# First entry with tokens on partitions, outputs finished at set steps, and squares and scale rows later at three entries

## The chip, the cores and the metric

The kernel runs on one core of one Trainium2 chip. The metric is the device time of one execution in microseconds. TensorE multiplies matrices (PE in the profile, PEld for its weight loads), VectorE (DVE) and GpSimd (POOL) do elementwise work, ScalarE (ACT) activations and copies, and SyncE (SP) issues nearly all transfers.

## The reference

A hybrid decoder layer on x of 1024 tokens by 1024 features, all float32, cut to its lines:

```python
x = x + 0.5 * swiglu(rms_norm(x, ffn1_norm), ffn1_w_gate, ffn1_w_up, ffn1_w_down)   # D_FF = 2816
h = rms_norm(x, mix_norm)
fq, fk, fv, f_logit, sq, sk, sv, g_fox, g_sb = split_columns(h @ w_in)
...                      # two causal token mixers, 8 heads of 64 each
merged = sigmoid(g_fox) * (y_fox @ w_branch_fox) + sigmoid(g_sb) * (y_sb @ w_branch_sb)
x = x + merged @ w_out
x = x + 0.5 * swiglu(rms_norm(x, ffn2_norm), ffn2_w_gate, ffn2_w_up, ffn2_w_down)
x = x + sigmoid(rms_norm(x, ple_norm) @ w_ple_gate) * (p @ w_ple_proj)
```

where `rms_norm(x, g) = x * rsqrt(mean(x*x, axis=-1) + 1e-6) * g`, and `swiglu` is `(silu(h @ w_gate) * (h @ w_up)) @ w_down`.

## The kernel before

**Layout.** x is handed over transposed, so that features lie on the 128 partitions (8 blocks k) and tokens along the free axis, in two halves of 512. Every operand of a product is split into a rounded high part (a ScalarE copy into fp32r) and a low part (a VectorE subtraction), and a product is three passes high-high, high-low, low-high: 12 matmuls of 128x512 for four blocks. The split of weights is `prep(n, m)`; its ScalarE and VectorE steps are in `split`.

**Products with combinations.** A stage with 2x2 blocks (feature halves by token halves) is done with seven products in place of eight. `make_up` does this for the two feed-forwards, the gates of the mixer and the last stage (the gated layer embedding, called PLE here). For weight block n there are products (n, 1) to (n, 7); B[1] and B[2] are the normalised operand of token half 0, `"12"` and 3 that of half 1, and 5, 6, 7, 4 are sums and differences, built by `combo_a` and `combo_b` (scale half 1 and split it), `combo_t`/`combo_l` (5), `combo_u`/`combo_s` (6, and 7), `combo_d`/`combo_e` (4). Block 0 is done without combinations (`plain(f, half, parts)`), while these are built. `up_order` is the fixed list of products; `products(F)` does what stands before it: (1,1), (1,2), plain for half 1. Then steps s = 0, 1, 2, ... follow the list, which begins (2,1), (1,5), (2,2), (1,6), (1,7), (2,6), (2,5), (1,3), (2,7), (1,4), (3,1), (2,4), (3,2). For the last stage it goes on with (3,6), (3,5), (3,7), (2,3), (3,3), (3,4), s = 13 to 18. At each step come the product, `evict` (bank copied or added into a result tile `E[n]`, activation), `begin(s)` and `prep` of the product four steps ahead.

**Order.** These stages stand in a manual schedule: each engine carries out its instructions in the order of the program text, and an instruction that waits holds up all behind it on its engine. Buffers come from named pools (`BUFS`: GF, RN, Q, KH, KL, Y, X 2 each, T 6, H and PT 4, WL and WH 3); a new tile waits until the last use of the one whose buffer it takes, also where that use stands later in the text of another engine.

**Norms.** `norm_sq` squares a feature block on ScalarE and adds it to an accumulator, on GpSimd mostly (line 187); `norm_sum` sums over partitions by matmuls with a column of ones (line 196) and takes the power -0.5 on GpSimd; `norm_row` (line 208) turns the result into a row over all partitions by transposes; `norm_mul` scales. At the first entry (`first_entry`) half 0's squares are summed by matmuls directly (line 190). At the other three entries (mixer, second feed-forward, last stage) squares and scaling are woven into the last down products by `up_step`, and `up_first` runs the first plain products.

**Last stage.** `ple_start` (lines 1539 to 1636): `fetch` loads p's projection and x for a 128-row tile into two buffers, `finish(n, i, ...)` multiplies, adds and sends out (lines 1559 to 1561). Finishes are put in a list `lag` and done at the next `evict`, after its own steps; each finish then fetches the next tile. `E[n]` takes buffers GF and RN for every n, two of each; line 1583 is the copy of (n,1) into GF, line 1585 that of (n,6), 1588 the add of (n,7).

Of the kernel before, what the change touches and what calls it, by code (L numbers as in the profile page):

```python
# [36 lines left out]
def tile_hybrid_decoder_layer(  # L37
    ctx: ExitStack,
    tc: tile.TileContext,
    x, p, ffn1_norm, ffn1_w_gate, ffn1_w_up, ffn1_w_down, mix_norm, w_in, forget_bias,  # L40
# [118 lines left out]
    gains = cp.tile([P, 4, KD], F32, name="gains")  # L159
    for i, gain in enumerate((ffn1_norm, mix_norm, ffn2_norm, ple_norm)):  # L160
        nc.scalar.dma_start(gains[:, i, :], gain[0])
# [14 lines left out]
    def norm_sq(N, k, eng=nc.gpsimd, ps=None):  # L176

        q = N["q"]
        if ps is None and "acc" not in N:
            d = N["acc"] = q["t"][0][:, N["half"], :]  # L180
            nc.scalar.activation(d, N["x"][:, k, :], AF.Square, scale=D ** -0.5)
            return
        q["n"] += 1
        d = q["t"][1][:, q["n"] % 2, :]
        nc.scalar.activation(d, N["x"][:, k, :], AF.Square, scale=D ** -0.5)  # L185
        if ps is None:
            eng.tensor_add(N["acc"], N["acc"], d)  # L187
            return
        for t in range(4):
            pe(nc.tensor.matmul(ps[:, t:t + 1], d[:, t * P:(t + 1) * P], ones1[:], start=(k == 0 and t == 0), stop=(k == KD - 1), skip_group_check=True))  # L190
# [37 lines left out]
    def norm_low(N, k, eng=nc.vector):  # L228
        B = N["B"][k // 4]
        eng.tensor_sub(B[:, 1, k % 4, :], N["x"][:, k, :], f(B[:, 0, k % 4, :]))  # L230

# [47 lines left out]
    def up_step(N, X, dst, F, i, t):  # L279
# [19 lines left out]
        elif i == 6:  # L299
            finished(X, dst, 1, t)  # L300
            if t == 0:
                norm_mul(N[0], 7)
            for k in ((0, 1, 2), (3, 4), (5, 6), (7,))[t]:
                norm_high(N[0], k)
            norm_sq(N[1], t, nc.vector if t == 3 else nc.gpsimd)
            for k in ((0, 1, 2), (3, 4), (5, 6), (7,))[t]:
                norm_low(N[0], k)

    def up_first(N, F):
# [12 lines left out]
        F.plain(1, 0)  # L322
        combos(F)
        products(F)
# [142 lines left out]
    def make_up(N, src, nm_, tags, first_fn, first_done=None, over=None):  # L467
# [17 lines left out]
        def plain(f_, half, parts=(0, 1), out=True):  # L485
# [5 lines left out]
            for kh in parts:  # L491
                hl, rb = hls[0, ((1, 2), (5, 4))[f_][kh]], B[("12", 3)[kh]] if half else whole(N[0]["B"][kh])
                for a, b in ((0, 0), (1, 0), (0, 1)):
                    for k in range(4):
                        pe(nc.tensor.matmul(ps[:], hl[:, a, k, :], rb[b](k), start=(i == 0), stop=(i == 23)))  # L495
                        i += 1
# [38 lines left out]
        def product(n, m, cols=slice(0, 512)):  # L535
# [9 lines left out]
            for a, b in ((0, 0), (0, 1), (1, 0)):  # L545
                for k in range(4):
                    pe(nc.tensor.matmul(ps[:, cols], hl[:, a, k, :], B[m][b](k)[:, cols], start=(first and i == 0), stop=(final and i == 11), skip_group_check=True))  # L547
                    i += 1
            return ps

        def whole(t):
            return lambda k: t[:, 0, k, :], lambda k: t[:, 1, k, :]

        def home(m):
            tag = tags["B"][m]
            if isinstance(tag, str):
                return whole(slot(tag, [P, 2, 4, 512], F32R))
            t = [slot(x_, [P, 2, 512], F32R) for x_ in tag]
            return lambda k: t[k // 2][:, k % 2, :], lambda k: t[2 + k // 2][:, k % 2, :]

        def xk(half, k):
            return norm_at(N[half], k)

        def high(m, k, src):
            nc.scalar.copy(B[m][0](k), src)

        def low(m, k, src, eng=nc.vector):
            eng.tensor_sub(B[m][1](k), src, f(B[m][0](k)))

        def combo_a(k):  # L570

            if k == 0:
                B[1], B[2] = (whole(t) for t in N[0]["B"])
                B[3] = home(3)
                B["12"] = home("12")
            norm_mul(N[1], k)
            norm_mul(N[1], k + 4)
            high("12", k, xk(1, k))
            high(3, k, xk(1, k + 4))

        def combo_b(k, eng=None):
            if eng is not None:
                low("12", k, xk(1, k), eng)
            else:
                low(3, k, xk(1, k + 4))

        def combo_t(k):

            if k == 0:
                B[5] = home(5)  # L590
            nc.vector.tensor_sub(xk(0, k), xk(1, k), xk(0, k))
            high(5, k, xk(0, k))

        def combo_l(k):
            low(5, k, xk(0, k))

        def combo_u(k):
            nc.vector.tensor_sub(xk(1, k), xk(1, k + 4), xk(1, k))
            nc.vector.tensor_sub(xk(1, k + 4), xk(1, k + 4), xk(0, k))
            if k == 0:  # L600
                B[6] = home(6)
            high(6, k, xk(1, k + 4))

        def combo_s(k, m):

            if m == 6:
                low(6, k, xk(1, k + 4))
                return
            if k == 0:
                B[7] = home(7)  # L610
            high(7, k, xk(1, k))
            low(7, k, xk(1, k))

        def combo_d(k):
            nc.vector.tensor_sub(xk(1, k), xk(0, k + 4), xk(1, k + 4))

        def combo_e(k):
            if k == 0:
                B[4] = home(4)
            high(4, k, xk(1, k))  # L620
            low(4, k, xk(1, k))
# [538 lines left out]
    def mix_start():  # L1160
# [47 lines left out]
        def begin(i, X):  # L1208
            if not Xs:
                Xs.extend(X)  # L1210
            up_begin(N, X, 1, F, i)

        def end():
# [17 lines left out]
            hT.extend([lambda a, k: B0[k // 4][:, a, k % 4, :], lambda a, k: B1[k // 4][a](k % 4)])  # L1231
# [163 lines left out]
    X = [slot("X", [P, KD, 512]) for _ in range(2)][::-1]  # L1395
# [3 lines left out]
    def first_entry(F):  # L1399

        def load_x(half):
            for k in range(KD):
                nc.sync.dma_start(X[half][:, k, :], xs[k, :, half * 512:half * 512 + 512])

        claim(X[1])
        load_x(0)
        nc.scalar.activation(stat([P, 1], "ss")[:], mhalf[:, 0:1], AF.Silu)
        F.load(0)
        load_x(1)
        F.load(1)  # L1410
        q = scratch()
        N.append(norm_begin(X[0], 0, 0, scratch()))
        N.append(norm_begin(X[1], 0, 1, q, ("Q", "Q", "KH", "KL")))
        ps = bank("sc")
        for k in range(KD):
            norm_sq(N[0], k, ps=ps)
        norm_pow(N[0], ps)
        norm_row(N[0], bank("av"))
        F.prep(0, 1)
        F.prep(0, 5)  # L1420
        for k in range(4):
            norm_mul(N[0], k)
            norm_high(N[0], k)
        for k in range(4):
            norm_low(N[0], k)
            norm_sq(N[1], k)
        for k in range(4, 8):
            norm_mul(N[0], k)
            norm_high(N[0], k)
        F.prep(0, 2)  # L1430
        F.prep(0, 4)
        for k in range(4, 8):
            norm_low(N[0], k)
        for k in range(4, 8):
            norm_sq(N[1], k, nc.gpsimd if k < 6 else nc.vector)
        F.plain(0, 0, (0,), False)
        F.plain(1, 0, (0,), False)
        F.plain(0, 0, (1,))
        norm_sum(N[1], bank("sc"))
        F.prep(1, 1)  # L1440
        F.prep(1, 2)
        F.sums(1, nc.vector)
        F.plain(1, 0, (1,))
        norm_row(N[1], bank("av"))
        F.prep(1, 5)
        F.load(2)
        combos(F)
        products(F)
# [222 lines left out]
```

## Time and profile before

| what | us |
|---|---|
| median of 3 runs (2272.24 to 2272.86) | 2272.28 |
| the profiled execution | 2271.59 |
| its span in the trace | 2269.9 |
| TensorE busy in the span | 2224.8 |
| first plain product starts | 23.11 |
| last TensorE product starts | 2262.34 |

Rows of the order of time read: start, length, engine, line, operation, output <- inputs, shape, how many were merged into the row, and in brackets the idle time before it and who ended it. SPq and ACTq are transfers being issued.

### The profile page before, as it was taken

How to read it: one execution, taken by the hardware profiler on the slowest of the kernel's cores; microseconds unless marked ns; L12 is line 12 of the kernel's file. 1: busy time of each engine (PE TensorE's matmuls, PEld its weight loads, DVE VectorE, ACT ScalarE, POOL GpSimd, SP SyncE). 2: the span in 40 equal slices, each digit the busy share in tenths (PEclk: the TensorE clock that was granted, in tenths of full speed). 3: DMA queues.
4: the chain of work that ended last, by engine and by line, in shares of the span. 5: the costliest groups of instructions: out<-in, count | busy, mean ns of one | idle time of the engine just before them, and what ended most of it. 6: DMA issues, size and time to landing. Idle time of an engine off the chain costs nothing.

```text
span 2269.9 us, 30559 instructions
## 1 busy us (share of the span) xinstructions
PE 2224.8 (98%) x11218; PEld 1888.9 (83%) x11218; DVE 1525.1 (67%) x2354; ACT 1000.0 (44%) x1791; POOL 832.1 (37%) x789
## 2 busy tenths in 40 slices
PE   7999999999999999999999999999999999999997
PEld 6888888888888898999898888887888888888886
DVE  5854545497888334666678885889655555778797
ACT  4433333343455435555566663245333333434444
POOL 2244444310021335566556664521544353200120
PEclk9999999999999999999999999999999999999999
DMA  4223232484332425333324466741423232655325
GB/s 139 79 96 113 93 116 93 153 314 150 127 133 79 136 87 148 93 94 84 88 54 97 117 200 204 259 149 56 139 79 130 79 131 79 249 198 189 130 96 201
DMA packets 197477, 298.04 MB, mean 131 GB/s; under 512 B 29000, under 2 KB 109128, under 8 KB 197328
## 3 DMA queue, kind: packets, MB, share of 16 engines
q1 hardware_dynamic: 196752, 296.08, 39.6%
q8 instruction: 88, 1.44, 0.3%
q14 instruction: 61, 0.50, 0.1%
q10 hardware_dynamic: 576, 0.02, 0.0%
HBM read 196.14 MB, written 83.13 MB: 123 GB/s over the span
## 4 chain that ended last, share of the span: by engine, by line
PE 84%; DVE 9%; ACT 2%; issue 2%; DMA 1%; POOL 0%; SPq 0%; DVEq 0%; ACTq 0%; POOLq 0%
PE ps L547 39%; PE ps L447 18%; PE ps L770 7%; PE ps L778 5%; PE ps L1373 4%; PE ps L1111 3%; PE ps L495 2%; PE ps L1085 2%; PE ps L1027 1%; PE ps L1026 1%; DVE H L106 1%; PE ps L932 1%; DVE H L230 1%; DVE PT L1093 1%; DVE X L221 1%
## 5 line engine op out<-in xcount | busy, mean ns | idle before, releaser
L447 PE MATMUL ps<-H,H 128*128 128x512 f32 x2184 | 498.1, 389 | 1.9 <-DVE X L455 1.2
L447 PEld LDWEIGHTS ps<-H,H 128*128 128x128 f32 x2184 | 409.3, 188 | 87.7 <-issue 3.0
L547 PE MATMUL ps<-H,WL 128*128 128x512 f32 x1152 | 273.5, 391 | 6.9 <-ACT GF L1585 6.8
L547 PEld LDWEIGHTS ps<-H,WL 128*128 128x128 f32 x1152 | 217.0, 189 | 53.2 <-ACT GF L1585 7.2
L187 POOL TENSOR_TENSOR PT<-PT,PT 128x512 f32<-128x512 f32 x41 | 55.3, 1348 | 425.2 <-ACT PT L185 424.1
L547 PE MATMUL ps<-H,Q 128*128 128x512 f32 x636 | 150.8, 389 | 0.0
L547 PEld LDWEIGHTS ps<-H,Q 128*128 128x128 f32 x636 | 119.4, 188 | 24.8
L455 DVE SCALAR_TENSOR_TENSOR X<-ps,X 128x512 f32<-128x512 f32 x168 | 108.5, 685 | 46.8 <-PE ps L447 46.7
L547 PE MATMUL ps<-X,WL 128*128 128x512 f32 (+1 forms) x588 | 138.7, 385 | 0.6 <-ACT RN L1611 0.6
L547 PE MATMUL ps<-H,PT 128*128 128x512 f32 x540 | 129.1, 389 | 0.6 <-DVE RN L1588 0.6
L547 PEld LDWEIGHTS ps<-X,WL 128*128 128x128 f32 x588 | 108.9, 188 | 22.8 <-ACT RN L1611 0.8
L139 POOL TENSOR_TENSOR WL<-RAW,WH 128x512 fp32r<-128x512 f32 (+1 forms) x84 | 98.3, 1192 | 68.3 <-ACT WH L129 43.6
L1093 DVE TENSOR_TENSOR PT<-ps,PT 128x512 fp32r<-128x512 f32 (+1 forms) x160 | 100.0, 627 | 31.0 <-ACT PT L1087 30.3
L547 PEld LDWEIGHTS ps<-H,PT 128*128 128x128 f32 x540 | 101.2, 188 | 21.9 <-DVE RN L1588 1.0
L770 PE MATMUL ps<-WH,H 128*128 128x256 f32 x768 | 116.1, 288 | 0.8 <-ACT RN L835 0.8
L778 PE MATMUL ps<-H,WH 128*128 128x512 f32 x384 | 114.9, 406 | 0.0
L1111 PE MATMUL ps<-PT,X 128*128 128x256 f32 (+1 forms) x640 | 102.4, 286 | 6.4 <-DVE PT L1093 5.5
L1087 ACT CAST PT<-ps 128x512 fp32r<-128x512 f32 (+1 forms) x160 | 87.1, 548 | 43.3 <-PE ps L1085 42.1
L1111 PEld LDWEIGHTS ps<-PT,X 128*128 128x128 f32 x640 | 90.3, 190 | 16.7 <-DVE PT L1093 10.3
L770 PEld LDWEIGHTS ps<-WH,H 128*128 128x128 f32 x768 | 101.4, 190 | 2.7 <-ACT RN L835 1.3
L348 POOL TENSOR_TENSOR PT<-GF,RN 128x512 f32<-128x512 f32 x20 | 33.6, 1682 | 188.8 <-DVE GF L680 188.8
L1039 POOL TENSOR_TENSOR T<-T,l 128x128 f32<-128x128 f32 (+3 forms) x64 | 73.2, 1147 | 72.2 <-DVE l L1038 69.9
(379 smaller groups left out, 4794.7 us busy)
## 6 DMA issues: line engine op xcount, KB each, us to landing
hidden<-PT SPq DMA_DIRECT2D x40, 512.0 KB, 3.1
WH<-in_ffn_w_gate_dram SPq DMA_DIRECT2D x38, 512.0 KB, 4.7
Q<-hidden SPq DMA_DIRECT2D x24, 512.0 KB, 6.5
hidden<-RN SPq DMA_DIRECT2D x22, 512.0 KB, 2.6
KH<-in_ffn_w_up_dram SPq DMA_DIRECT2D x20, 512.0 KB, 6.1
KL<-in_ffn_w_up_dram SPq DMA_DIRECT2D x20, 512.0 KB, 6.9
T<-in_ffn_w_down_dram SPq DMA_DIRECT2D x20, 512.0 KB, 6.0
GF<-hidden SPq DMA_DIRECT2D x14, 512.0 KB, 7.5
```

The source lines that it names most:

```text
L139: ins = eng_lo.tensor_sub(lo[part], raw[part], f(hi[part]))
L187: eng.tensor_add(N["acc"], N["acc"], d)
L447: pe(nc.tensor.matmul(groups[g][t][:], wt[:, b, k, t * P:(t + 1) * P], act[:, a, k, :], start=(fresh and n == 0), stop=(i in (6, 1, 4) and ...
L455: nc.vector.scalar_tensor_tensor(xs, groups[g][t][:], scale, xs, ALU.mult, ALU.add)
L547: pe(nc.tensor.matmul(ps[:, cols], hl[:, a, k, :], B[m][b](k)[:, cols], start=(first and i == 0), stop=(final and i == 11), skip_group_che ...
L770: pe(nc.tensor.matmul(ps[:, :n], hT[t // 4](a, k)[:, (t % 4) * P:(t % 4 + 1) * P], w[k // 4][b][:, k % 4, :n], start=(i == 0), stop=(i == ...
L778: pe(nc.tensor.matmul(ps[:], w[a][:, k, :], hT[half](b, k), start=(i == 0), stop=(i == 23)))
L1039: nc.gpsimd.tensor_mul(T[:, :n], T[:, :n], l[:].broadcast_to([P, n]))
L1087: high = nc.scalar.copy(pt[:, 0, :width], ps[:, :width])
L1093: ins = nc.vector.tensor_sub(pt[:, 1, :width], ps[:, :width], f(pt[:, 0, :width]))
L1111: pe(nc.tensor.matmul(o, lh, r, start=(kpair == c and i == 0), stop=(kpair == 0 and i == 3)))
L1373: pe(nc.tensor.matmul(ps[:], w[a][:, k, :], yT[g][b][:, k, half * 512:half * 512 + 512], start=(i == 0), stop=(i == 11)))
```

## The change

x is handed over a second time in its natural layout (`x_rows`), and the first norm's gain as a plain row.

- *First entry.* `rows_stat` squares a tile of 128 tokens by 1024 features in one ScalarE step that also sums it, GpSimd takes the power; `rows_mul` scales by token and by the gain, which `spread` has copied to all partitions by two products with a row of ones; `rows_high` and `rows_low` transpose the scaled tile on TensorE (`turn`, eight transposes of 128x128) and split it out of PSUM. Half 1's tiles are transposed in `combo_a`. `busy(4)` issues four matmuls of zeros ahead of the transposes. The order of splits, plain products and combinations is written out anew. In this entry the combinations work on pieces of 128 tokens by four feature blocks, and `combo_t` and `combo_d` take half 0's operand back from its high and low parts, with one more step each. All its low parts are on VectorE; three were on GpSimd.
- *Three entries.* In `up_step` the squares of half 1's blocks 0 to 3 go to four places of their own (a third tile in Y), and their adds come on VectorE at the end, after the low parts of half 0. In `up_first` the two parts of plain(0, 0) come together ahead of `norm_sum`, and `norm_row` comes after the first part of plain(1, 0).
- *Last stage.* `lag` is gone. A table `AT` says after which step each fetch and finish stands, each fetch has a named buffer (Q, KH or T), and `E[2]` goes to Y.

```diff
+    def spread(gB):
+        ones = slot("T", [1, P])
+        nc.vector.memset(ones[:], 1.0)
+        banks = [bank("sc") for _ in range(2)]
+        for i, ps in enumerate(banks):
+            pe(nc.tensor.matmul(ps[:], ones[:], gB[0:1, i * 512:i * 512 + 512], start=True, stop=True))
+        for i, ps in enumerate(banks):
+            nc.vector.tensor_copy(gB[:, i * 512:i * 512 + 512], ps[:])
+    def rows_stat(N, t, tag, first=False):
+        xt = N["x"][:, t, :]
+        h = N["h"][t] = slot(tag, [P, D])
...
+        nc.scalar.activation(h[:], xt, AF.Square, scale=D ** -0.5, accum_out=ss[:])
...
+        nc.gpsimd.tensor_tensor(rs[:], ss[:], mhalf[:, 0:1], ALU.pow)
+    def rows_mul(N, t):
+        nc.vector.scalar_tensor_tensor(N["h"][t][:], N["x"][:, t, :], N["r"].pop(t)[:], N["g"][:], ALU.mult, ALU.mult)
+    def turn(h, b, ps):
+        for c in range(4):
+            k = 4 * b + c
+            pe(nc.tensor.transpose(ps[:, c * P:(c + 1) * P], h[:, k * P:(k + 1) * P], identf[:]))
+        return ps[:].rearrange("p (c t) -> p c t", c=4)
...
     def up_first(N, F):
         F.load(2)
-        F.plain(0, 0, (0,))
-        norm_sum(N[1], bank("sc"))
         F.prep(0, 5)
         F.prep(0, 4)
+        F.plain(0, 0, (0, 1), False)
+        norm_sum(N[1], bank("sc"))
         F.prep(1, 1)
         F.prep(1, 2)
         F.sums(1, nc.vector)
-        F.plain(0, 0, (1,))
+        F.silu(0, 0)
+        F.prep(1, 5)
+        F.plain(1, 0, (0,))
         norm_row(N[1], bank("av"))
-        F.prep(1, 5)
-        F.plain(1, 0)
+        F.plain(1, 0, (1,), False)
         combos(F)
+        F.silu(1, 0)
         products(F)
...
+            if rows():
+                nc.vector.tensor_sub(d, w(j, 0), f(cut(B[1], 0, j)))
+                nc.vector.tensor_sub(d, d, f(cut(B[1], 1, j)))
...
     def first_entry(F):
+        X = [slot("X", [P, 4, D]) for _ in range(2)]
+        load_x(0)
         nc.scalar.activation(stat([P, 1], "ss")[:], mhalf[:, 0:1], AF.Silu)
+        gB = slot("PT", [P, D])
+        nc.scalar.dma_start(gB[0:1, :], ffn1_norm[0].unsqueeze(0))
+        busy(0)
+        spread(N[0]["g"])
...
+        for t in range(4):
+            rows_stat(N[0], t, ("PT", "WL", "WL", "PT")[t], True)
+            rows_mul(N[0], t)
+        busy(4)
+        rows_high(N[0], 0, ps1)
+        rows_high(N[0], 1, ps1)
+        rows_low(N[0], 0)
+        F.prep(0, 1)
+        rows_high(N[0], 2, ps2)
+        rows_low(N[0], 1)
+        rows_high(N[0], 3, ps2)
+        rows_low(N[0], 2)
+        rows_stat(N[1], 0, "Y")
+        rows_low(N[0], 3)
+        F.prep(0, 2)
...
-                E[n] = [slot(t, [P, 2, 512]) for t in ("GF", "RN")]
+                E[n] = [slot(t, [P, 2, 512]) for t in (("Y", "Y") if n == 2 else ("GF", "RN"))]
...
+        AT = {4: [(fetch, 0, 1, "Q")], 5: [(finish, 0, 0)], 6: [(fetch, 1, 0, "KH"), (fetch, 1, 1, "T")], 7: [(finish, 0, 1)], 8: [(fetch, 2, 1, "Q")],
+              9: [(finish, 1, 0)], 10: [(finish, 1, 1), (fetch, 3, 0, "KH")], 11: [(fetch, 3, 1, "T")], 12: [(finish, 2, 1)], 13: [(fetch, 2, 0, "Q"), (finish, 3, 0, h0)],
+              16: [(finish, 3, 1, h1)], 17: [(finish, 2, 0), (finish, 3, 0, h1)]}
```

More of the change, by code (lines that the diff above doesn't have):

```diff
@@ L556, in home @@
             if isinstance(tag, str):
[L557 to L573, printed above, removed]
+                return slot(tag, [P, 2, 4, 512], F32R)
@@ L1595, in evict @@
                     nc.scalar.activation(e1[:, 0, :], e1[:, 0, :], AF.Sigmoid)
-                    finish(n, 0, e1, h0, more=False)
             elif m == 3:
```

348 lines of the change are left out of this document (210 added, 138 removed).

## The prediction

> **What bounds the kernel now.** I read the page first, for what is busy, and then who TensorE (PE) waits for (columns: total us, times, longest).
>
> ```profile
> span 2269.9 us, 30559 instructions
> PE 2224.8 (98%) x11218; PEld 1888.9 (83%) x11218; DVE 1525.1 (67%) x2354; ACT 1000.0 (44%) x1791; POOL 832.1 (37%) x789
> PE ps L547 <- ACT GF L1585: 6.8, 1, 6.8
> PE ps L190 <- ACT PT L185: 5.3, 1, 5.3
> PE ps L196 <- DVE PT L187: 3.3, 4, 0.9
> PE ps L547 <- ACT Y L657: 1.4, 2, 0.8
> ```
>
> TensorE is busy 98% of the span; only 2269.9 - 2224.8 = 45 us are left, besides products that run slow. What the change touches are three of these waits and the start. The start, in order of time (start, us, engine, line):
>
> ```profile
> 4.65 1.36 ACT L185 ACTIVATE PT<-X 128x512 f32<-128x512 f32 x2 [0.50 <-DMA X<-in_x_dram]
> 5.33 13.81 PE L190 MATMUL ps<-ones,PT 128*128 128x1 f32 x64 [5.33 <-ACT PT L185]
> 23.11 10.24 PE L495 MATMUL ps<-H,WL 128*128 128x512 f32 x32 [1.49 <-ACT H L226]
> 24.30 2.49 DVE L230 TENSOR_TENSOR H<-X,H 128x512 fp32r<-128x512 f32 x4
> 63.60 2.88 PE L547 MATMUL ps<-H,PT 128*128 128x512 f32 x12
> 89.57 2.88 PE L547 MATMUL ps<-X,Q 128*128 128x512 f32 x12
> 36.00:40.00 4.00, 2.91 (x10) 1.95 (x11) 2.39 (x4) 0.61 (x2) 0.00 (x0) 0.77 0.00 0
> 40.00:45.00 5.00, 5.00 (x13) 4.03 (x14) 3.28 (x5) 1.20 (x3) 1.03 (x1) 0.50 0.00 0
> 75.42:89.57 14.15, 14.03 (x61) 11.29 (x61) 14.00 (x23) 5.75 (x11) 0.00 (x0) 1.00 0.08 20
> ```
>
> For 13.8 us TensorE only sums squares, and the first useful product starts at 23.11. The last three rows are stretches of time (window, length, then busy PE, PEld, DVE, ACT, POOL, granted clock, DMA): VectorE (DVE) is busy 14.00 of 14.15 us up to 89.57, where product (1,4) of the first feed-forward begins. So VectorE, not TensorE, sets the pace of the start until then; after that TensorE runs without a wait. The gain of the new start is how much earlier (1,4) comes. The 0.77 and 0.50 rows show that the sparse stretch at 33 to 38 us was paid with half clock.
>
> The last stage:
>
> ```profile
> 2172.31 2.88 PE L495 MATMUL ps<-H,WL 128*128 128x512 f32 x12
> 2175.98 1.05 PE L196 MATMUL ps<-ones,PT 128*128 128x1 f32 x8 [0.79 <-DVE PT L187]
> 2185.63 5.60 PE L547 MATMUL ps<-H,PT 128*128 128x512 f32 x24
> 2209.33 1.22 DVE L1559 TENSOR_TENSOR GF<-GF,Y 128x1024 f32<-128x1024 f32 x1
> 2210.11 2.88 PE L547 MATMUL ps<-T,WL 128*128 128x512 f32 x12
> 2215.00 0.58 ACT L1583 COPY GF<-ps 128x512 f32<-128x512 f32 x1 [6.31 <-DMA out_dram<-GF]
> 2219.75 4.37 PE L547 MATMUL ps<-H,WL 128*128 128x512 f32 x12 [6.76 <-ACT GF L1585]
> 2223.96 2.89 PE L547 MATMUL ps<-T,PT 128*128 128x512 f32 x12
> 2257.32 3.03 PE L547 MATMUL ps<-H,PT 128*128 128x512 f32 x12 [0.56 <-DVE RN L1588]
> 2260.19 1.59 PE L547 MATMUL ps<-X,WL 128*128 128x256 f32 x12
> 2266.54 0.42 DVE L1560 TENSOR_TENSOR RN<-RN,Y 128x256 f32<-128x256 f32 x1
> 2254.06 7.40 DMA KH<-p_proj
> ```
>
> The copy of (2,1) into GF waits 6.31 us until the output of tile (0,0) has left that buffer. Everything behind it on ScalarE (ACT) waits too, and TensorE stands 6.76 us at (1,7); that product then takes 2223.96 - 2219.75 = 4.21 us instead of 2.72 (2226.68 - 2223.96 is a normal one), so 1.49 us go to the clock.
>
> **The change part by part.** Prices: a 512-element VectorE step follows the last one after (2.49 - 0.69)/3 = 0.60 us, a 1024 one after 1.2; ScalarE 0.62 (follows after 0.52) and 1.06; the row reads:
>
> ```profile
> L568 DVE TENSOR_TENSOR X<-X,X 128x512 fp32r<-128x512 f32 x16 | 11.0, 689 | 0.7
> L671 ACT ACTIVATE GF<-GF 128x1024 f32<-128x1024 f32 x20 | 21.2, 1060 | 87.3 <-DVE GF L664 87.3
> L1037 ACT ACTIVATION_READ_ACCUMULATOR T<-T,m 128x1 f32 x64 | 12.0, 188 | 0.0
> L106 DVE TENSOR_TENSOR X<-ps,X 128x256 fp32r<-128x256 f32 x32 | 13.3, 417 | 18.6 <-ACT X L105 18.4
> DMA to landing us min/median/max: 1.8/2.1/4.0
> gqk<-in_k_norm_dram SPq DMA_DIRECT2D x1, 0.2 KB, 6.4
> 2158.24 0.60 PE L208 MATMUL ps<-identf,rs 128*128 128x128 f32 x4
> 2158.60 13.88 PE L447 MATMUL ps<-H,H 128*128 128x512 f32 x60
> ```
>
> *The start.* Removed: 64 matmuls of L190, the two row transposes, 16 squares of 512. Added on ScalarE: eight squares of 1024 with their sum, 1.06 + 0.19 = 1.25 us each; on TensorE 64 transposes at (2158.60 - 2158.24)/4 = 0.09 us, 5.8 us in all, and two fp32 products that spread the gain; on VectorE eight 1024-wide scalings at 1.2, and four more steps each in t and d, which rebuild their operand from high and low. The x loads carry the same bytes (2 MB for each half) on the same queue, and tile 0 is there near 5 us as now, so loads cost nothing. The weight load F.load(2), moved a little on the load queue, waits for WH buffers that are free near 26 us and is wanted first at prep(2,1), past 40. ScalarE's squares and GpSimd's powers (1.0 us each) for tiles 0 to 3 are done before VectorE can use them.
>
> What starts the chain is the gain row: its DMA stands on ScalarE's queue behind the first activation (ended 4.1 us). Small loads landed 1.8 to 4.0 us after issue (the gains rows, answer on that tile) and 6.4 us on the full queue; I take 4.0, thus 8.1, bounds 6 to 10.5. The two spread products have no row: from 2 x 0.23 (as fp32r) to 3.4; I take 1.7, since an fp32 product stands as two instructions. Two copies of 0.6 give 11.4. From there VectorE has, in program order up to the low part that product (2,5) needs: 71 steps of 0.60 (8 lows of rows, 14 weight lows, 16 in combination t and l with their extra steps, and so on) = 42.9, eight scalings = 9.6, eight 256-wide lows at 0.34 = 2.7: together 55.2. It stands for about 6 us more, where a difference must go to ScalarE for its high part and come back (0.8 each at four u steps, 1.3 at prep(2,1), 0.12 at each dependent pair). So (2,5) has its last operand at 11.4 + 55.2 + 6 = 72.6; four products and the next bank's release bring (1,3) to 74.5, and two products of 2.72 bring (1,4) to 79.9: 9.7 us before 89.57. That VectorE now has no GpSimd (POOL) adds beside it is in these prices.
>
> From this I take off 2.0 us: between 12.6 and 17.7 TensorE does only eight transposes (0.72 us) in each 1.2 us, after a gap, then waits for the lows, as sparse as 33 to 38 us is now, after which it ran at 0.50. If some 16 products run at half clock, that is 16 x 0.227 = 3.6 us, of which 1.6 pass while it would wait for lows anyway. Start: **-7.7**, bounds -4 and -11.5. The Trainium skill ("TensorE: Matmul & The Clock Gate", section "Part 4: PE-mode transpose") says that transposes do not count as activity for the clock; by it the four matmuls of busy(4) before them would not keep the clock up, and the loss of 2.0 would stand. No run here shows it yet.
>
> *Three entries.* plain(0,0) now has both parts ahead of norm_sum, 5.44 us of cover where 2.72 stood, so the 0.79 us (four such waits, 3.3 in all, 0.9 of them at the start) go. The three GpSimd adds become VectorE steps: four dependent adds of 0.72 after the last low, which end near 2177.8, when TensorE arrives (2172.31 + 5.44). VectorE reaches the combinations at the same time as now, 2183.0, so TensorE, 0.8 to 0.9 early, meets small waits, some 0.35 in all, at the first plain product of half 1 and at (1,7), whose operands come no earlier than now. Mixer and second entry **-0.45 and -0.5**, last entry -0.8 into the next part; bounds 0 and -0.9 each.
>
> *Last stage.* (2,1) goes to Y, whose two buffers are free (the third tile of squares is done at 2177.8). The 6.76 falls to the 0.8 that (1,7) has always behind the copy of (1,6) (row L657), and the 1.49 of clock and 0.56 at (3,3) are due to go. But each finish is two 1024 steps, 2.4 us of VectorE, and finishes 0 to 3 no longer run while TensorE stands. VectorE is free for the sums of weight 2 at 2209. Up to the add of evict(3,2): 36 steps = 21.8, four finishes = 9.6, and 4.4 in which ScalarE's part is waited for: 2244.8. Behind that add are on ScalarE its sigmoid 0.62, a weight split 0.52 and the copy of (3,6), which frees the bank for (3,7): 2246.6, where TensorE could start at 2244.3. So 2.3 us are waited there, likewise 1.2 at (3,2) behind finish(0,1), and 0.7 at (3,3): with 0.9 at (1,7) and 0.2 of small ones 5.3. Now 15 products take 2260.19 - 2210.11 = 50.1 us where 15 x 2.72 = 40.8 would do: 9.3 lost now, 5.3 after: -4.0. The end after (3,4) keeps its VectorE chain (two finishes of 2.4 and 1.4, four of 0.42): 6.8 now, much the same after. With the entry's 0.8: **-4.8**, bounds -2.5 and -9.5.
>
> Sum: -7.7 - 0.45 - 0.5 - 4.8 = -13.4. The profiled execution took 2271.59 (span 2269.9 and 1.7 around it), 0.7 below the median of 2272.28; I keep that offset: 2272.3 - 13.4 = **2258.9 us**.
>
> **The rivals.**
> (A) The clock holds through the transposes: the 2.0 stay won, 2256.9. For it: the clock column is 1.00 from 5 to 36 us in spite of small gaps. Against: the 0.50 row.
> (B) The finishes cost TensorE nothing, because VectorE has more slack than I count: of 5.3 only the 0.9 at (1,7) remains, 4.4 more, 2254.5. For it: all of today's 4.9 us of finishing is done before 2214.2 and TensorE shows no VectorE wait after it until 2257; against: VectorE was given 6.8 us there.
> (C) The new fetch points are late. Each finish has three or four steps of 2.72 after its fetch, 8.2 us; the worst landing is 7.4 (p_proj into KH). If landings take 9 to 10 us under the output traffic, VectorE blocks some 1 to 2 us at three or four finishes: 4 us given back, 2262.9. Nearly the old wait in another place.
> (D) Slower. The row layout works in pieces of four times 128 elements, 52 VectorE steps of 512 in the chain of the start. I price them as contiguous. If such a step took 1.0 us, as with GpSimd beside it, the start would lose 52 x 0.4 = 21 us and the kernel would end at 2279.7; it decides from 13.4/52 = 0.26 us a step on. Against: the 256-wide row L106 above, which writes pieces of 64 elements, costs 417 ns, no more than any other 256-wide step here.
> (E) The pieces do what they say but the gains cancel: within 0.2%.
>
> **How the numbers follow.** 0.2% is 4.5 us, about what a measurement can tell from no change. Chances: forecast 0.44, A 0.18, B 0.18, C 0.11, D 0.07, E 0.02. A and B together, with the gain row at 6 us, reach 2252; C with half of the start's gain lost (bound -4) reaches 2266. These ends leave out D and little else: 2252 to 2266. Faster by over 0.2% means below 2267.7: forecast, A, B and C, 0.91; same 0.02; slower 0.07.
>
> **What would show it.** Right: L190 gone, the first plain product at about 18 us, (1,4) near 82, VectorE nearly without idle from 11 to 72; the wait for norm_sum gone at three entries; no wait over 1 us at (1,7) of the last stage and clock 1.00 there, but short waits of TensorE at (3,2), (3,7) and (3,3) for ScalarE or VectorE. Wrong: the gain row landing after 11 us; VectorE steps on 128-wide pieces clearly over 0.69; VectorE waiting for a fetched p_proj or x_end for over 1 us; a wait for a Y, Q, KH or T buffer on the load queue that holds up weights. If (1,4) comes at 90 or later, the whole reading of the start falls.

## The result, and the profile after

| | us |
|---|---|
| kernel before, median of 4 runs (2271.49 to 2272.86) | 2272.26 |
| changed kernel, median of 4 runs (2257.54 to 2259.86) | 2258.51 |
| ratio, with its 95% interval | 0.994 (0.9923 to 0.9957) |
| profiled execution of the changed kernel | 2258.84 |

The change makes the kernel 13.7 us faster; 2258.9 was predicted. The total came out almost exactly, but none of its three terms did: their errors cancelled, and that is luck. From the page of the changed kernel come its span and, from its list of waits (total us, times, longest), those of TensorE (PE) that matter:

```profile
span 2257.1 us, 30539 instructions
PE ps L241 <- DMA PT<-in_ffn_norm_dram: 7.7, 1, 7.7
PE ps L613 <- ACT GF L1720: 3.8, 2, 3.2
PE ps L613 <- DVE WL L106: 2.0, 1, 2.0
```

The 6.8, 5.3 and 3.3 us of before are gone. What stands in their place is a wait for the gain row, one of 3.2 us in the last stage, and one of 2.0 us in the start. The start in order of time, and its last stretch (window, length, busy PE, PEld, DVE, ACT, POOL, granted clock, DMA):

```profile
7.72 3.75 PE L241 MATMUL ps<-PT,T 1*128 1x512 f32 x4 [7.72 <-DMA PT<-in_ffn_norm_dram]
11.41 1.89 PE L255 MATMUL ps<-T 128*128 128x512 bf16 x4
12.30 1.28 DVE L270 SCALAR_TENSOR_TENSOR PT<-X,rt,PT 128x1024 f32<-128x1024 f32 x1
19.97 2.11 PE L561 MATMUL ps<-H,WL 128*128 128x512 f32 x8 [0.81 <-ACT H L284]
74.75 1.53 PE L613 MATMUL ps<-H,WL 128*128 128x512 f32 x4 [2.02 <-DVE WL L106]
76.56 4.11 PE L613 MATMUL ps<-T,WL 128*128 128x512 f32 x12 [0.27 <-DVE Y L775]
80.50 2.90 PE L613 MATMUL ps<-X,WL 128*128 128x512 f32 x12
83.25 2.88 PE L613 MATMUL ps<-X,Q 128*128 128x512 f32 x12
70.00:83.00 13.00, 10.71 (x39) 7.84 (x39) 12.86 (x21) 5.43 (x10) 0.00 (x0) 0.87 0.15 40
```

The first plain product starts at 19.97 instead of 23.11, and (1,4) at 83.25 instead of 89.57: 6.3 us won. VectorE (DVE) is busy 12.86 of 13 us, so it is still the bound. New is that TensorE's clock falls to 0.87 behind the 2.02 us wait at (2,5), and product (1,3) takes 80.50 - 76.56 = 3.94 us instead of 2.72.

The last entry and the last stage (against 2172.31, 2185.63, 2210.11, 2219.75 and 2260.19 before):

```profile
2162.59 5.60 PE L561 MATMUL ps<-H,WL 128*128 128x512 f32 x24
2174.89 5.60 PE L613 MATMUL ps<-H,PT 128*128 128x512 f32 x24
2199.38 2.88 PE L613 MATMUL ps<-T,WL 128*128 128x512 f32 x12
2202.93 3.02 PE L613 MATMUL ps<-H,WL 128*128 128x512 f32 x12 [0.68 <-ACT GF L1720]
2234.45 0.68 DVE L1726 TENSOR_TENSOR GF<-GF,ps 128x512 f32<-128x512 f32 x1
2235.17 0.63 ACT L1728 ACTIVATE GF<-GF 128x512 f32<-128x512 f32 x1 [6.43 <-DVE GF L1726]
2236.21 0.58 ACT L1720 COPY GF<-ps 128x512 f32<-128x512 f32 x1
2236.84 11.30 PE L613 MATMUL ps<-H,PT 128*128 128x512 f32 x36 [3.17 <-ACT GF L1720]
2247.97 1.59 PE L613 MATMUL ps<-X,WL 128*128 128x256 f32 x12
2230.00:2240.00 10.00, 6.83 (x25) 5.18 (x24) 8.73 (x11) 2.66 (x5) 0.00 (x0) 0.80 0.66 236
```

The wait for norm_sum is gone: the entry takes 2174.89 - 2162.59 = 12.30 us, where it took 13.32. At (1,7) 0.68 us stand where 6.76 stood. The chain predicted for (3,7) is there link by link: VectorE's add of (3,2) at 2234.45, behind the finishes; ScalarE's sigmoid L1728, which has waited 6.43 us for it; the copy of (3,6); then (3,7). The three products from 2236.84 on took 11.1 us; the clock is 0.80 in the last row and 0.88 from 2240 to 2252. At the end, 2269.9 - 2257.1 = 12.8 us are won: 6.3 in the start, 3.2 at the three entries, 2.1 from (1,6) on, and 1.2 in the long stretches between, where no edit stands.

### The profile page after: what moved, and what is told of

The parts are those of the page before. It is cut to its first block, busy times and chain, and to the rows that moved or that the text cites. A ratio compares the mean times of both kernels' runs of the same rounds, so it can differ in the third digit from the quotient of the medians.

```text
span 2257.1 us, 30539 instructions
## 1 busy us (share of the span) xinstructions
PE 2218.3 (98%) x11210; PEld 1881.7 (83%) x11210; DVE 1518.7 (67%) x2371; ACT 1005.1 (45%) x1805; POOL 808.2 (36%) x782
## 4 chain that ended last, share of the span: by engine, by line
PE 87%; DVE 8%; ACT 2%; issue 2%; DMA 1%; POOL 0%; SPq 0%; DVEq 0%; ACTq 0%; POOLq 0%
PE ps L613 39%; PE ps L513 20%; PE ps L885 7%; PE ps L893 5%; PE ps L1488 4%; PE ps L1226 3%; PE ps L561 3%; PE ps L1200 2%; PE ps L1142 1%; PE ps L1141 1%; PE ps L1047 1%; DVE PT L1208 1%; DVE H L106 1%; DVE RN L1104 1%; DVE GF L1104 1%
## 5 line engine op out<-in xcount | busy, mean ns | idle before, releaser
L187 POOL TENSOR_TENSOR PT<-PT,PT 128x512 f32<-128x512 f32 x27 | 34.9, 1294 | 405.6 <-ACT PT L184 404.7
L1226 PEld LDWEIGHTS ps<-PT,X 128*128 128x128 f32 x640 | 90.2, 190 | 16.6 <-DVE PT L1208 10.1
```

Of the source, the lines that this page charges most:

```text
L1226: pe(nc.tensor.matmul(o, lh, r, start=(kpair == c and i == 0), stop=(kpair == 0 and i == 3)))
```

## The experiments

Times below are medians; each stands beside runs of the kernel before on the same chip (2272.2 or 2273.0). Differences from the changed kernel are small: the executions of `gain_first`, `keep_clock`, `finish_later` and `all_three` all lie below its 2257.54 to 2259.86, though only the interval of `all_three` lies clear of its interval; those of `warm_start`, `gate_later` and `lows_gpsimd` overlap its range and those of `no_busy` end at its edge, so there the traces carry the reading, not the time.

**The parts alone.** Three kernels, each the kernel before with one part of the change.

`start_alone`:

```diff
-    X = [slot("X", [P, KD, 512]) for _ in range(2)][::-1]
...
+        X = [slot("X", [P, 4, D]) for _ in range(2)]
...
+            rows_stat(N[0], t, ("PT", "WL", "WL", "PT")[t], True)
+            rows_mul(N[0], t)
```

> The kernel before with the new first entry alone; the three entries and the last stage are the old ones. Theory 1 (the trace of the changed kernel: product (1,4) of the first feed-forward begins at 83.25 instead of 89.57 us, and nothing later depends on how it got there): 6.3 us below the kernel before, (1,4) at 83.2 to 83.3, and every later product earlier by the same 6.3. Theory 2 (the prediction's term): 7.7 below. Theory 3 (some of the 6.3 is eaten later, because the old stages have fixed waits on transfers): less than 5.5 below.

Measured 2264.66 us, 7.5 below (ratio 0.9966, 0.9954 to 0.9979); five executions spread from 2263.2 to 2267.6. Around (2,5):

```profile
74.98 1.20 PE L606 MATMUL ps<-H,WL 128*128 128x512 f32 x4 [1.94 <-DVE WL L106]
76.78 3.01 PE L606 MATMUL ps<-T,WL 128*128 128x512 f32 x12 [0.60 <-DVE Y L768]
82.35 2.88 PE L606 MATMUL ps<-X,Q 128*128 128x512 f32 x12
```

(1,4) comes at 82.35, 0.9 earlier than in the changed kernel, although (2,5) waits as long and resumes 0.2 later: here the clock did not fall. The same text of this entry, with the same wait, lost 0 us in one execution and 1.1 in the other. The interval holds theories 1 and 2 alike and the upper end of theory 3; what the traces show is that the 6.3 contains one draw of the clock.

`entries_alone`:

```diff
-            norm_sq(N[1], t, nc.vector if t == 3 else nc.gpsimd)
+            N[0]["adds"].append(norm_sq(N[1], t, None))
...
-        F.plain(0, 0, (0,))
-        norm_sum(N[1], bank("sc"))
...
+        F.plain(0, 0, (0, 1), False)
+        norm_sum(N[1], bank("sc"))
```

> The kernel before with the edits of the three entries alone (adds of four squares on VectorE at the end, norm_sum after both parts of the first plain product, scale row after the first part of the next). Theory 1 (the shifts read off the trace of the changed kernel: 1.05, 1.13 and 1.02 us at the three entries, all kept): 3.2 us below the kernel before. Theory 2 (the prediction's terms, 0.45, 0.5 and 0.8): 1.75 below. Theory 3 (the last entry's part is lost again at the 6.76 us wait of the old last stage, since that wait ends with a transfer): 2.2 below.

Measured 2267.58 us, 4.6 below (0.9978, 0.9968 to 0.9987); the span is 3.5 shorter. Theory 1 is inside the interval (3.0 to 7.3), the prediction's 1.75 is not, nor is theory 3.

`last_alone`:

```diff
-        lag = []
...
+                E[n] = [slot(t, [P, 2, 512]) for t in (("Y", "Y") if n == 2 else ("GF", "RN"))]
...
+                for fn, *args in AT.get(s, ()):
+                    fn(*args)
```

> The kernel before with the new last stage alone (outputs finished at set steps, own home for the third pair). Theory 1 (the trace of the changed kernel: between (1,6) and the end of the span 12.8 - 10.7 = 2.1 us are won; TensorE waits about 3 us at (3,7) and runs the next 36 products at a granted clock near 0.85): 2.1 us below the kernel before, with that wait and that clock there. Theory 2 (the prediction's term without the entry): 4.0 below. Theory 3 (the wait at (3,7) belongs to the earlier arrival from the new entry and not to the finishes): no wait over 1.5 us at (3,7), and 6 to 8 us below.

Measured 2268.39 us, 3.8 below (0.9981, 0.9972 to 0.999); the span is 3.2 shorter.

```profile
2247.78 9.95 PE L547 MATMUL ps<-H,PT 128*128 128x512 f32 x36 [3.19 <-ACT GF L1569]
```

The wait at (3,7) is there with the old entries too, 3.19 us, so theory 3 falls: it does not come from the new entry. This time the three products behind it took 9.8 us, not 11.1. The interval (2.3 to 6.4) holds the prediction's 4.0 and just leaves out the 2.1 of theory 1, whose wait and falling clock are there all the same. The three medians add up to 16.0 and the three spans to 15.1, against 13.7 and 12.8 together. Two things in the traces make up 2.2 of the 2.3 us between the spans. `start_alone` lost no clock at (1,3), 1.1 us. And in it the second feed-forward's entry, which it has in the old text, no longer waits for norm_sum: from the first plain product to the first product behind the plain ones it takes 1539.73 - 1527.44 = 12.29 us, where the kernel before takes 1548.80 - 1535.37 = 13.43, so 1.1 us are counted in two parts. Why that wait went is not shown. Besides, stretches with the same text drift both ways: (1,4) begins at 88.11 in `last_alone` and at 89.57 in the kernel before, with the same start.

**What sets the pace of the start.** `gain_first`:

```diff
-        nc.scalar.activation(stat([P, 1], "ss")[:], mhalf[:, 0:1], AF.Silu)
         gB = slot("PT", [P, D])
         nc.scalar.dma_start(gB[0:1, :], ffn1_norm[0].unsqueeze(0))
+        nc.scalar.activation(stat([P, 1], "ss")[:], mhalf[:, 0:1], AF.Silu)
+        load_gains()
```

(`load_gains` issues the transfers of the three other gains, which stood ahead of all this.)

> The changed kernel, but the gain row's transfer is the first on ScalarE's queue, ahead of the table load and of the three other gains. It should land near 3 us instead of 7.72, so the two spread products end near 7 and the first scaling, which then waits for the first power (ended 6.72 us) and the copies, begins near 8.3 instead of 12.30. Theory 1 (VectorE's chain sets the pace of the start from the first scaling to product (1,4), so all of it comes earlier by the same amount): (1,4) near 79.3, 4.0 us below the changed kernel, that is 17.8 below the kernel before. Theory 2 (loads and the x tiles of half 1, or the weights, then come last): about 1 to 2 us below the changed kernel, with VectorE idle for a transfer. Theory 3 (TensorE's clock takes it back, as at 70 to 83 us where the granted clock was 0.87): (1,4) earlier by less than 3, with a clock below 0.9 somewhere from 14 to 80 us.

```profile
2.38 3.75 PE L243 MATMUL ps<-PT,T 1*128 1x512 f32 x4 [2.38 <-DMA PT<-in_ffn_norm_dram]
70.74 1.27 PE L615 MATMUL ps<-H,WL 128*128 128x512 f32 x4 [2.02 <-DVE WL L106]
80.94 2.88 PE L615 MATMUL ps<-X,Q 128*128 128x512 f32 x12
```

2254.33 us median (0.9917, 0.9903 to 0.993), 4.2 below the changed kernel. (2,5) comes 74.75 - 70.74 = 4.0 us earlier, with the same 2.02 us wait. The first scaling comes even 5.3 us earlier, at 6.95, but the next three wait 0.45 us each for GpSimd's powers. From the first low part on (13.37 instead of 17.09, 3.7 earlier), sixty us of VectorE's chain moved as one piece. That is theory 1, and it shows the prediction's bound. But in this execution (1,4) is only 2.3 earlier: behind (2,5) the clock took 1.7 more than in the changed kernel (theory 3). The other executions took 2251.8 to 2254.9; the fastest has a mean granted clock of 1.00, the others 0.998.

`warm_start`:

```diff
+    def warm(n):
+        ps, t = bank("av"), identf[:].bitcast(BF16)
+        for _ in range(n):
+            pe(nc.tensor.matmul(ps[:, 0:256], t[:, 0:P], t, start=True, stop=True))
...
+        warm(36)
         spread(N[0]["g"])
```

> The changed kernel with 36 idle matmuls (bf16, 256 wide) ahead of the two spread products, in the 7.7 us in which TensorE waits for the gain row. Theory 1 (the 3.75 us of the spread products are fp32 products at half clock: the four bf16 matmuls of busy(4) that follow took 1.89 us for 2048 columns, 16 of 256 in a warm stretch 1.92 us for 4096): the spread products take 1.9 us, busy(4) about 1.0, the first scaling begins 1.9 us earlier than 12.30, and the chain up to (2,5) with it: 1.9 us below the changed kernel, apart from what the clock does behind (2,5). Theory 2 (3.75 us is what such one-row fp32 products cost at any clock): no change, the first scaling at 12.0 to 12.6.

```profile
7.60 1.95 PE L241 MATMUL ps<-PT,T 1*128 1x512 f32 x4
9.48 1.04 PE L255 MATMUL ps<-T 128*128 128x512 bf16 x4
10.38 1.29 DVE L275 SCALAR_TENSOR_TENSOR PT<-X,rt,PT 128x1024 f32<-128x1024 f32 x1
72.57 1.21 PE L618 MATMUL ps<-H,WL 128*128 128x512 f32 x4 [2.00 <-DVE WL L106]
82.84 2.88 PE L618 MATMUL ps<-X,Q 128*128 128x512 f32 x12
```

The spread products take 1.95 us instead of 3.75, the first scaling begins 1.92 earlier and (2,5) 2.2 earlier: theory 1. Yet the time is 2257.99 us (0.9937, 0.9921 to 0.9954), 0.5 below the changed kernel, because (1,4) comes at 82.84, only 0.4 earlier: the clock again. So 2 us won in the start are lost within 10 us of the place where TensorE waits for VectorE. Executions spread over 4.5 us.

`no_busy`:

```diff
-        busy(0)
...
-        busy(4)
```

> The changed kernel without the four matmuls of zeros ahead of the first transposes. Theory 1 (transposes do not keep the clock up, as the Trainium skill has it in TensorE: Matmul & The Clock Gate, Part 4: PE-mode transpose; the four matmuls did): the products from 19.97 to 27 us run at about half clock, 2 to 4 us more at product (1,4), 2260 to 2263 us. Theory 2 (what TensorE does at 13.6 to 20 us counts, or the clock was up already from the two spread products): granted clock 1.00 from 14 us on, (1,4) within 0.5 us of 83.25 apart from what the stretch at 70 to 83 us does, no change in time that can be measured.

```profile
13.78 1.97 PE L275 MATMUL ps<-identf,PT 128*128 128x128 f32 x8 [2.17 <-DVE PT L270]
17.97 1.04 PE L275 MATMUL ps<-identf,PT 128*128 128x128 f32 x8
19.91 2.11 PE L561 MATMUL ps<-H,WL 128*128 128x512 f32 x8 [0.91 <-ACT H L284]
2237.05 8.78 PE L613 MATMUL ps<-H,PT 128*128 128x512 f32 x36 [3.19 <-ACT GF L1718]
2245.67 1.59 PE L613 MATMUL ps<-X,WL 128*128 128x256 f32 x12
```

2257.04 us (0.9931, 0.9916 to 0.9945): theory 2. From 11.6 to 19.9 us TensorE did nothing but 32 transposes, and the first eight matmuls of the plain product then took 2.11 us, exactly as with the four matmuls of zeros. The clock rose during the transposes: the first eight took 1.97 us, the last eight 1.04, and the trace's first record of the clock, at full, stands at 16.93 (in the changed kernel at 17.40). The Trainium skill's rule that transposes are no activity for the clock (TensorE: Matmul & The Clock Gate, section "Part 4: PE-mode transpose") would have these matmuls at half speed; this trace does not agree. The last row, the same 3.19 us wait at (3,7), had no clock loss behind it here: 2245.67 - 2237.05 = 8.6 us for three products.

**Waits and the clock.** `keep_clock`:

```diff
+                if a and (n, m) == (2, 5) and rows():
+                    warm(16)
...
+                if (n, m) == (3, 7):
+                    warm(24)
```

> The changed kernel with idle matmuls (bf16, 256 wide, of a constant tile, into a bank that nobody reads) in the two places where TensorE waits longest: 16 ahead of the third pass of (2,5) of the first feed-forward, where it waits 2.02 us for VectorE, and 24 ahead of (3,7) of the last stage, where it waits 3.17 us for ScalarE. No other engine's work changes, and the waits end when they ended. Theory 1 (the clock falls because TensorE stands still there): granted clock 1.00 at 70 to 83 us and at 2230 to 2250 us, (1,3) takes 2.72 instead of 3.94 us and the 36 products from (3,7) on take 8.2 instead of 11.1; about 4 us below the changed kernel, at most 0.5 of it lost to the idle matmuls themselves. Theory 2 (the clock there falls for another reason, or idle matmuls don't count): no gain, clock as before, 2258 to 2260 us.

```profile
72.48 1.92 PE L260 MATMUL ps<-identf 128*128 128x256 bf16 x16
74.65 1.21 PE L620 MATMUL ps<-H,WL 128*128 128x512 f32 x4 [0.26 <-DVE WL L106]
82.03 2.88 PE L620 MATMUL ps<-X,Q 128*128 128x512 f32 x12
2235.89 8.79 PE L620 MATMUL ps<-H,PT 128*128 128x512 f32 x36 [0.56 <-ACT GF L1727]
2244.52 1.59 PE L620 MATMUL ps<-X,WL 128*128 128x256 f32 x12
```

2255.28 us (0.9924, 0.9909 to 0.9939), 3.2 below the changed kernel, with four executions within 1.1 us. (2,5) resumes at 74.65, as before (74.75), but (1,4) comes at 82.03; the three products from (3,7) on take 8.6 us. The granted clock is 1.00 in all stretches. No other engine's work changed, so in the changed kernel the clock falls because TensorE stands still, and idle matmuls prevent it: theory 1. The time from (1,3)'s start to (1,4)'s start, two products, 5.57 us at full speed, in all traces that have the 2.0 us wait there:

| kernel | from (1,3) to (1,4), us |
|---|---|
| start_alone | 5.57 |
| no_busy | 6.46 |
| changed kernel | 6.69 |
| gate_later, finish_later, lows_gpsimd | 7.11, 7.17, 7.17 |
| gain_first, warm_start | 8.40, 8.47 |
| keep_clock, all_three (wait filled) | 5.58, 5.57 |

The same 2 us wait costs 0 to 2.9 us more behind it. The granted clock tells why the cost differs, here in `gain_first`:

```profile
71.73:78.55 6.82, 6.29 (x15) 4.74 (x15) 5.54 (x10) 1.87 (x4) 0.00 (x0) 0.50 0.23 74
```

Half clock comes in stretches of 3.41 us or twice that: 75.43 to 78.84 in the changed kernel, 71.73 to 78.55 in `gain_first`, 73.69 to 80.52 in `warm_start`, none here in `start_alone`. In the 3.41 us ahead of each of these falls TensorE stood still for 2.0 us. In `start_alone`, steps of 3.41 us counted on from its first record of the clock at 16.70 have a border at 74.73. It cuts the wait in two, 1.7 us before it and 0.25 behind it, and the clock stayed.

At (3,7) it is the same: in `no_busy` a border at 2235.59 cuts the 3.19 us into 1.73 and 1.46, and nothing was lost, while 2.39 us within one step cost the changed kernel half clock from 2236.06 to 2242.89. The text of the start does not set where the borders fall (74.73 in `start_alone`, 75.43 in the changed kernel), so what one execution pays for such a wait is luck. In the six traces with 3.15 to 3.19 us of waiting at (3,7), the three products behind took 8.6, 9.65, 9.8, 9.9, 9.9 and 11.1 us. Idling is not all that counts: in `warm_start` the clock also fell at 12.25, behind 3.41 us with 1.2 us of standing still and one-row products, matmuls of zeros and transposes in the rest; that stays open.

The Trainium skill (TensorE: Matmul & The Clock Gate, section "Part 1: The HAM clock gate (the "warmup" mystery)") says that activity is judged in windows of about 3.4 us which run freely and do not start with the program; by that the cost of one wait depends on where it falls in a window, and the stretches of 3.41 us and the waits cut in two agree. That section lets the clock fall after an idle window; here 2.0 us of standing still within 3.41 were enough, and the measurement decides.

**The last stage.** `gate_later`:

```diff
-                if n == 3:
-                    nc.scalar.activation(e1[:, 0, :], e1[:, 0, :], AF.Sigmoid)
...
+        def gate32():
+            e1 = E[3][0]
+            nc.scalar.activation(e1[:, 0, :], e1[:, 0, :], AF.Sigmoid)
...
-              ... 13: [(fetch, 2, 0, "Q"), (finish, 3, 0, h0)],
+              ... 13: [(fetch, 2, 0, "Q"), (gate32,)], 14: [(finish, 3, 0, h0)],
```

> The changed kernel with one ScalarE step moved: the sigmoid of (3,2), which waits for VectorE, stands one step later, behind the copy of (3,6) that frees the bank for (3,7); the finish that needs it goes from step 13 to 14. VectorE's order is otherwise the same. Theory 1 (the 3.17 us at (3,7) is ScalarE's queue, blocked by that sigmoid, and nothing else is late there): the wait at (3,7) falls below 1 us; the clock is then kept at 1.00, and 3.2 + 3.0 us less what (3,3) waits for VectorE: 3 to 5 us below the changed kernel. Theory 2 (VectorE's sum of steps is the bound; the sigmoid only shows it): the wait turns up at (3,3), 2.4 us or more, with its clock loss, and the time falls by 1 us at most.

```profile
2200.96 2.88 PE L613 MATMUL ps<-T,WL 128*128 128x512 f32 x12
2235.02 5.60 PE L613 MATMUL ps<-H,PT 128*128 128x512 f32 x24
2243.17 3.06 PE L613 MATMUL ps<-H,PT 128*128 128x512 f32 x12 [2.54 <-DVE RN L1723]
2246.06 1.59 PE L613 MATMUL ps<-X,WL 128*128 128x256 f32 x12
```

2257.25 us (0.9932, 0.9917 to 0.9947), 1.3 below the changed kernel. (3,7) starts without a wait, and 2.54 us turn up at (3,3), for VectorE: theory 2 in its main point. ScalarE's blocked sigmoid only handed on what VectorE's sum of steps had set. Its clock loss did not come with it here. From (1,6) on, which this execution began 1.6 us later than the changed kernel's, (3,4) comes after 2246.06 - 2200.96 = 45.1 us instead of 48.6. But 2.5 of these 3.5 us are the changed kernel's clock loss behind (3,7): `no_busy`, with the same last stage and no such loss, takes 2245.67 - 2199.61 = 46.1. The moved sigmoid itself won 1.0, as theory 2 has it.

`finish_later`, gate_later's sigmoid and:

```diff
-              9: [(finish, 1, 0)], 10: [(finish, 1, 1), (fetch, 3, 0, "KH")], ... 12: [(finish, 2, 1)],
+              9: [(finish, 1, 0)], 10: [(fetch, 3, 0, "KH")], ... 14: [(finish, 1, 1), (finish, 2, 1)],
```

> The changed kernel with the sigmoid of (3,2) later as in the run beside this one and with three finishes moved: finish(0,1) from step 7 to 8, finish(1,1) and finish(2,1) to step 14, behind everything that (3,7) needs, finish(3,0) of the first half to 15; the fetch of (2,0) goes into T. Theory 1 (the finishes ahead of (3,7) on VectorE are what TensorE pays for in this stage): no wait over 1 us between (1,7) and (3,4), granted clock 1.00, product (3,4) starts 5 to 6.5 us earlier than 2247.97, and the end, which then has VectorE's finishes behind it, comes 4 to 6 us earlier. Theory 2 (VectorE's work only moves to the end, where it is bound too): (3,4) earlier, but the end by less than 2 us.

```profile
2200.16 2.88 PE L613 MATMUL ps<-T,WL 128*128 128x512 f32 x12
2240.51 3.01 PE L613 MATMUL ps<-H,PT 128*128 128x512 f32 x12 [1.13 <-DVE RN L1723]
2243.36 1.59 PE L613 MATMUL ps<-X,WL 128*128 128x256 f32 x12
```

2254.0 us (0.9917, 0.99 to 0.9933), 4.5 below the changed kernel, four executions within 0.5 us. From (1,6) to (3,4) it takes 2243.36 - 2200.16 = 43.2 us instead of 48.6, 5.4 less, and (3,7) follows (3,5) without a wait; 1.13 us remain at (3,3). Against `no_busy`'s 46.1, which lost no clock, it is 2.9 less. Theory 1, but for that 1.13: finishes ahead of (3,7) on VectorE, of 2.4 us each, were what TensorE paid for.

**GpSimd as a helper.** `lows_gpsimd`:

```diff
-        F.b(0, nc.vector)
+        F.b(0, nc.gpsimd)
...
-            F.b(2 + i, nc.vector)
+            F.b(2 + i, nc.gpsimd)
```

> The changed kernel with four 512-element low parts of half 1 in the first entry on GpSimd instead of VectorE, as three of them stood in the kernel before. Theory 1 (GpSimd takes work off VectorE, which is the bound there): 4 x 0.60 = 2.4 us less on VectorE, so the 2.02 us wait at (2,5) goes, and with it the clock loss behind it: 2 to 4 us below the changed kernel. Theory 2 (VectorE's steps stretch while GpSimd runs one, as the 1.78 us step at 2226.76 beside GpSimd's at 2226.70 did, 1.1 us for one GpSimd step): VectorE gains 2.4 and loses up to 4.4: from no change to 2 us slower than the changed kernel.

```profile
29.27 3.73 POOL L649 TENSOR_TENSOR X<-Q,X 128x512 fp32r<-128x512 f32 x2
31.77 1.85 DVE L649 TENSOR_TENSOR T<-Q,T 128x256 fp32r<-128x256 f32 x2
33.54 1.78 DVE L576 TENSOR_TENSOR RAW<-KH 128x512 f32<-128x512 f32 x1
76.70 1.20 PE L613 MATMUL ps<-H,WL 128*128 128x512 f32 x4 [2.01 <-DVE WL L106]
```

2259.78 us (0.9944, 0.9927 to 0.996), 1.3 above the changed kernel: theory 2. VectorE's steps beside GpSimd's took 1.85 and 1.78 us instead of 0.76 and 0.69, and (2,5) comes 2.0 later, 0.4 of it because the gain row landed later. Moving four steps away, 2.4 us of VectorE, cost VectorE about 4, as an estimate: the 2.4 and the 1.6 us that (2,5) lost besides.

**The edits that helped, together.** `all_three`: gain_first, the idle matmuls at (2,5) alone, and finish_later.

> The changed kernel with the three edits that each helped: the gain row's transfer first, 16 idle matmuls ahead of the third pass of (2,5), and the later sigmoid and finishes of the last stage (no idle matmuls there). Theory 1 (the edits act at different places and add up): 4.0 for the gain row, 1.2 to 3.0 for the clock at 70 to 83 us, 4.5 for the last stage, so 9 to 11 us below the changed kernel, 2247.5 to 2249.5 us, with granted clock 1.00 in every stretch and executions closer together than the 2.3 us of the changed kernel. Theory 2 (the gain row's 4.0 is partly given back at another wait): 2250 to 2252 us.

```profile
78.18 2.88 PE L622 MATMUL ps<-X,Q 128*128 128x512 f32 x12
2237.88 1.59 PE L622 MATMUL ps<-X,WL 128*128 128x256 f32 x12
```

2248.9 us (2248.3 to 2249.35), ratio to the kernel before 0.9899 (0.9884 to 0.9913): 9.6 below the changed kernel, which is theory 1. (1,4) is at 78.18, 5.1 earlier than in the changed kernel, and (3,4) at 2237.88, 10.1 earlier. This version beats both kernels.

## Why the prediction was right, and where it was not

*The start, -7.7.* The trace has -6.3, the part alone -7.5 (4.8 to 10.5). The bound was read rightly: the chain follows its first VectorE steps (`gain_first`, `warm_start`). Inside, several terms were off and partly cancelled. The gain row landed at 7.72 (8.1 taken), but by luck: its transfer was issued at 2.27 and not behind the activation, and took 5.4 us to land, not 4.0. The spread products were the term mis-sized: 1.7 us taken, with no row behind it, 3.75 measured, since TensorE was still at half speed; warm it is 1.95. The sum 8.1 + 1.7 + 1.2 is 11.0, where 11.4 was written; the first scaling came at 12.30. The chain from there to (2,5)'s last operand took about 62.4 us where 55.2 + 6 was counted. The steps were counted rightly (71 of 512 elements, eight of 1024 and eight of 256 are in the trace); the 1.2 us more are waits and hand-overs, 0.46 of it for a power of half 1 from GpSimd. The 2.0 us for half clock at the transposes did not occur: the clock was low, but rose during them, and the first plain products ran at full speed, without busy(4) too. A loss of 1.1 us occurred instead at (1,3), behind the 2.02 us wait at (2,5), which the prediction had in its sum as a late operand but did not price for the clock. One loss of clock was priced that did not come, and one came that was not priced.

*Three entries, -0.45, -0.5 and -0.8.* Measured 1.02 at the last entry, and 1.05 and 1.13 at the other two. The step that failed is "small waits, some 0.35 in all": there are none. And removing a wait of 0.79 us wins more than 0.79, because the rows before and after it now overlap: 2162.59 + 5.60 = 2168.19, while the next row begins at 2168.04. The entry went from 13.32 to 12.30.

*Last stage, -4.0.* In the trace of all parts together -2.1, alone -3.8 (2.3 to 6.4). Of the 5.3 us of new waits, 4.05 came: 0.68, 0.20 and 3.17 at (1,7), (3,2) and (3,7), against 0.9, 1.2 and 2.3. The wait at (3,3) was predicted at 0.7 and has no row of its own. The mechanism was right and the place of the largest wait too. What was left out is the clock behind (3,7): 11.1 us for three products that took 8.6 in `no_busy`, 2.5 us. Without it the stretch from (1,6) to (3,4) takes `no_busy`'s 46.1 us, 4.0 less than the 50.1 of before, which is the prediction's number. The prediction had itself charged 1.49 us of clock to the old 6.76 us wait, and did not ask the same of the new one.

*The sum.* Start and last stage fell short by 1.4 and 1.9 us. The entries gave 1.45 more than forecast, and 1.2 us came in between: from (1,4) to the last entry 2082.74 us became 2079.34, and only 2.18 of these 3.40 are the two entries. That the total met the forecast is luck.

*The rivals.* A (the clock holds through the transposes) had the outcome, no loss at the plain products, but not the ground: its clock column of 1.00 from 5 us on says nothing up to 27.92, where the first record of the clock in the trace of before stands, and that kernel's first 32 plain matmuls took 10.24 us, 0.32 each, where 0.227 is normal. The 2 us of A were lost elsewhere. B (finishes cost nothing) falls with the 3.17 us and with finish_later. C (late fetches) did not show in the changed kernel: VectorE waits for no transfer in the last stage. D (128-wide pieces at 1.0 us) fell: the steps rebuilt from 128-wide pieces took no more than contiguous ones, as this row from the start of the changed kernel shows.

```profile
38.97 0.69 DVE L699 TENSOR_TENSOR RN<-Q,H 128x512 f32<-128x512 f32 x1
```

Open: why the start alone takes the wait out of the second entry, and where the 1.2 us in the untouched stretches come from.

## What to carry to other kernels

Price a TensorE wait twice: by its length, and by the clock behind it, here 0 to 3 us for a wait of 2 to 3 us and nothing for a single wait of 1.6 us. Where such a wait cannot be removed, fill it with idle matmuls, which made the time both shorter and steadier. Where one engine sets the pace for a whole stage, its first step is worth as much as any in the stage, until the next wait takes over: a row of 4 KB issued ahead of three others was worth 4 us, and moving steps to GpSimd brought (2,5) later instead of earlier.

## What was not expected of the hardware

- The clock column read 1.00 from the start, while the first products ran at half speed: four bf16 matmuls of 512 columns took 1.89 us at 11.41, but 1.04 at 9.48 behind 36 idle matmuls, and 3.75 against 1.95 us for the spread products. The traces have no record of the clock ahead of its first rise (17.40 us in the changed kernel, 27.92 in the kernel before), and the column shows 1.00 there. The durations of equal products tell what the column did not.
- A VectorE step of 0.69 us took up to 1.78, and a pair of 0.76 us 1.85, while GpSimd worked on two operands.
- A transfer of one row issued at 0.80 us and first on its queue landed at 2.38; issued at 2.27 behind three others it landed at 7.72.
